# Seven half-size products instead of eight for gate and up in a float32 decoder trunk on TensorE

## The chip, the cores and the metric

The kernel runs on one core of a Trainium2 chip. TensorE multiplies a stationary operand of 128 x 128 with a moving operand of up to 512 columns and adds into PSUM. VectorE, ScalarE and GpSimd work beside it, each with a queue of its own, and the queue of SyncE issues most transfers. The metric is the device time of one execution in microseconds, as the median of several runs.

## The reference

The input x has 512 positions and 1024 features. There are two layers. Each adds a half SwiGLU stage, a mixer (retention and dilated attention in layer 0, gated linear attention in layer 1), and a second half SwiGLU stage; a last norm follows. All is float32. The change touches the four SwiGLU stages:

```python
def _swiglu(h, wg, wu, wd):
    return (jax.nn.silu(h @ wg) * (h @ wu)) @ wd
...
    for l in range(DEPTH):
        h = _rmsnorm(x, ffn_pre_norm[l])
        x = x + 0.5 * _swiglu(h, ffn_pre_w_gate[l], ffn_pre_w_up[l], ffn_pre_w_down[l])
...
```

wg and wu are 1024 x 2816, wd is 2816 x 1024.

## The kernel before

Activations lie transposed: x is eight tiles of 128 features x 512 positions that stay in SBUF. The hidden width of 2816 is 22 tiles of 128, or 11 pairs of tiles. To keep float32 accuracy each operand is cut into a high half (a float32r copy, made on ScalarE) and a low half (the difference, made on VectorE), and each 128 x 128 by 128 x 512 product is three matmuls into the same PSUM tile: high by high, high by low, low by high. `mm3` (L121) issues the three; they are L124, L125 and L126 in the profile.

Weights come through one ordered plan (`run`, L756). `weights` (L77) takes the next tile and keeps LOOK = 3 more ahead: `load_w` (L83) transfers 512 KB on SyncE's queue, casts the high half `whi` on ScalarE (L89) and subtracts for the low half `wlo` on VectorE (L90). `whi` and `wlo` have four buffers each.

A SwiGLU stage (`ffn`, L292) works in two phases. For each of 22 tiles `proj_t` (L242) makes the gate tile and then the up tile, each 8 x 3 = 24 matmuls of 512 columns on x scaled by the norm's gain only (`xgh`, `xgl`, made by `scaled`, L165). `glu` multiplies both by `rrow`, the row of reciprocal norms per position, takes Silu, multiplies, and cuts the result into `act` halves. The row is not needed before `glu`, so the first projections run while it is made: `squares` (L182) sums x squared on GpSimd while the stage before ends, `stats_cols` (L220) and `stats_rows` (L224) are hooked in after the first two projections (third and fourth in the first stage). `rows` (L205) spreads it with two small `diag` matmuls. Then come the eight down tiles: `down` (L331) adds 22 products x 3 matmuls in one PSUM tile, `x` is updated (L326), and the next stage's scaled copy is made at once. The last output tile of the program runs in two halves of 256 columns (`last_half`, L339), so that the first half's final norm and stores run beside the second half.

Who comes first on an engine is set by the layer that records the program: it lists the instructions engine by engine, in an order of its own that keeps to what depends on what. Every engine then works through its list in that order.

## Time and profile before

| | |
|---|---|
| median of 3 runs | 1969.83 us (1969.54 to 1972.41) |
| the profiled execution | 1968.25 us |
| its span in the profile | 1966.3 us |
| TensorE busy, matmuls | 1949.1 us (99%), 8822 records |
| VectorE / ScalarE / GpSimd busy | 898.9 / 611.6 / 97.4 us |
| granted TensorE clock | 0.998 of full speed |
| HBM read | 179.89 MB, 93 GB/s over the span |

Matmuls are pipelined: a record's duration reaches into the next ones, so the time of a matmul is read from the distance between two starts. A few per cent of matmul records can be missing. Idle time of an engine that is off the path costs nothing.

### The profile page before, as it was taken

What the parts mean: (1) busy time and instruction counts of PE and PEld (TensorE: products, weight loads), DVE (VectorE), ACT (ScalarE), POOL (GpSimd) and SP (SyncE); (2) the same over time, 40 slices, a digit from 0 to 9 for tenths busy, and PEclk for the clock granted to TensorE, in tenths of its full rate; (3) what the DMA queues carried; (4) which work ended last, traced back from release to release, by engine and by line L of the source; (5) the groups of instructions that cost most, each with busy time, mean ns of one, the idle gap of its engine ahead of it and who ended that gap; (6) DMA issues with size and microseconds to landing.
All of it is one profiled execution on the core that took longest, in us unless ns stands there. A gap on an engine that the chain in (4) does not pass through costs nothing.

```text
span 1966.3 us, 21475 instructions
## 1 busy us (share of the span) xinstructions
PE 1949.1 (99%) x8822; PEld 1595.4 (81%) x8822; DVE 898.9 (46%) x1238; ACT 611.6 (31%) x813; POOL 97.4 (5%) x69
## 2 busy tenths in 40 slices
PE   8999999999999999999999999999999999999998
PEld 7888888877777888888888888888788888888887
DVE  6444433544565544443334444333456564444323
ACT  5333322233332332322233323222424243333221
POOL 1000001100001200000110000011000020000010
PEclk9999999999999999999999999999999999999999
DMA  5232233421121323222332332233222133223222
GB/s 173 97 97 97 94 98 92 140 81 57 54 70 49 118 96 97 97 94 96 95 102 97 97 97 96 89 99 104 91 84 67 55 117 97 97 97 95 92 95 73
DMA packets 54548, 183.38 MB, mean 93 GB/s; under 512 B 6177, under 2 KB 8481, under 8 KB 54450
## 3 DMA queue, kind: packets, MB, share of 16 engines
q1 hardware_dynamic: 51408, 177.76, 28.0%
q10 hardware_dynamic: 3042, 4.26, 0.7%
q8 instruction: 69, 1.13, 0.2%
q14 instruction: 29, 0.24, 0.0%
HBM read 179.89 MB, written 2.10 MB: 93 GB/s over the span
## 4 chain that ended last, share of the span: by engine, by line
PE 98%; issue 0%; DVE 0%; DMA 0%; POOL 0%; ACT 0%; POOLq 0%; DVEq 0%; SPq 0%
PE pj L124 31%; PE pj L126 30%; PE pj L125 30%; PE sc L520 1%; PE o L548 1%; PE sc L199 1%; PE sc L595 0%; PE tp L536 0%; PE sc L217 0%; PE o L752 0%; PE o L745 0%; PE sc L734 0%; DMA wraw<-in_w_gu 0%; PE tp L604 0%; PE o L124 0%
## 5 line engine op out<-in xcount | busy, mean ns | idle before, releaser
L89 ACT CAST whi<-wraw 128x1024 fp32r<-128x1024 f32 (+1 forms) x341 | 352.1, 1033 | 1112.1 <-PE pj L125 670.2
L124 PE MATMUL pj<-xgh,whi 128*128 128x512 f32 x1704 | 677.4, 398 | 6.9 <-ACT whi L89 6.9
L126 PE MATMUL pj<-xgh,wlo 128*128 128x512 f32 x1704 | 664.8, 390 | 0.0
L125 PE MATMUL pj<-xgl,whi 128*128 128x512 f32 x1704 | 664.6, 390 | 0.0
L90 DVE TENSOR_TENSOR wlo<-wraw,whi 128x1024 fp32r<-128x1024 f32 (+1 forms) x341 | 412.6, 1211 | 297.2 <-ACT whi L89 296.2
L124 PEld LDWEIGHTS pj<-xgh,whi 128*128 128x128 f32 x1704 | 320.6, 188 | 83.2 <-issue 12.1
L126 PEld LDWEIGHTS pj<-xgh,wlo 128*128 128x128 f32 x1704 | 320.2, 188 | 67.7 <-DVE wlo L90 0.8
L125 PEld LDWEIGHTS pj<-xgl,whi 128*128 128x128 f32 x1704 | 320.7, 188 | 64.3 <-issue 1.0
L124 PE MATMUL pj<-acth,whi 128*128 128x512 f32 (+1 forms) x726 | 277.8, 383 | 0.0
L125 PE MATMUL pj<-actl,whi 128*128 128x512 f32 (+1 forms) x726 | 277.7, 383 | 0.0
L126 PE MATMUL pj<-acth,wlo 128*128 128x512 f32 (+1 forms) x726 | 277.7, 383 | 0.0
L303 DVE TENSOR_TENSOR us<-pj,rrow 128x512 f32<-128x512 f32 x88 | 60.8, 691 | 272.4 <-PE pj L126 272.4
L124 PEld LDWEIGHTS pj<-acth,whi 128*128 128x128 f32 x726 | 136.4, 188 | 26.8
L126 PEld LDWEIGHTS pj<-acth,wlo 128*128 128x128 f32 x726 | 136.4, 188 | 26.5
L125 PEld LDWEIGHTS pj<-actl,whi 128*128 128x128 f32 x726 | 136.4, 188 | 26.5
L189 POOL TENSOR_TENSOR sqa<-sqa,sq 128x512 f32<-128x512 f32 x41 | 71.3, 1738 | 1412.4 <-issue 795.4
L301 DVE TENSOR_TENSOR gs<-pj,rrow 128x512 f32<-128x512 f32 x88 | 60.8, 691 | 173.7 <-PE pj L126 173.7
L117 ACT CAST acth<-us 128x512 fp32r<-128x512 f32 x88 | 54.9, 624 | 61.0 <-DVE us L304 61.0
L304 DVE TENSOR_TENSOR us<-us,gs 128x512 f32<-128x512 f32 x88 | 60.9, 692 | 9.4 <-ACT gs L302 0.8
L118 DVE TENSOR_TENSOR actl<-us,acth 128x512 fp32r<-128x512 f32 x88 | 60.3, 685 | 4.9 <-ACT acth L117 4.8
L326 DVE SCALAR_TENSOR_TENSOR x<-pj,x 128x512 f32<-128x512 f32 x31 | 21.4, 692 | 88.3 <-PE pj L126 88.3
L302 ACT ACTIVATE gs<-gs 128x512 f32<-128x512 f32 x88 | 55.2, 628 | 4.2 <-DVE gs L301 4.2
(164 smaller groups left out, 1170.1 us busy)
## 6 DMA issues: line engine op xcount, KB each, us to landing
wraw<-in_w_gu SPq DMA_DIRECT2D x176, 512.0 KB, 3.4
wraw<-in_w_down SPq DMA_DIRECT2D x64, 448.0 KB, 3.2
wraw<-in_w_down SPq DMA_DIRECT2D x32, 512.0 KB, 3.4
wraw<-in_w_dqk SPq DMA_DIRECT2D x8, 512.0 KB, 3.4
wraw<-in_w_rqk SPq DMA_DIRECT2D x8, 512.0 KB, 3.4
wraw<-in_w_eo SPq DMA_DIRECT2D x8, 512.0 KB, 3.6
wraw<-in_w_gr SPq DMA_DIRECT2D x8, 512.0 KB, 3.4
wraw<-in_w_gv SPq DMA_DIRECT2D x8, 512.0 KB, 3.5
```

The costliest lines, as they stand in the source:

```text
L89: self.halved = nc.scalar.copy(out=hi[:, :cols], in_=raw[:, :cols]).ins
L90: nc.vector.tensor_tensor(out=lo[:, :cols], in0=raw[:, :cols], in1=hi[:, :cols].bitcast(F32), op=ALU.subtract)
L117: nc.scalar.copy(out=hi, in_=src)
L118: nc.vector.tensor_tensor(out=lo, in0=src, in1=hi.bitcast(F32), op=ALU.subtract)
L124: mm(out, lhsT=w[0], rhs=x[0], start=first, stop=False)
L125: mm(out, lhsT=w[0], rhs=x[1], start=False, stop=False)
L126: self.last = mm(out, lhsT=w[1], rhs=x[0], start=False, stop=last).ins
L189: nc.gpsimd.tensor_tensor(out=self.sqacc, in0=self.sqacc, in1=sq, op=ALU.add)
L301: nc.vector.tensor_tensor(out=gs, in0=g, in1=self.rrow, op=ALU.mult)
L302: nc.scalar.activation(out=gs, in_=gs, func=AF.Silu)
L303: nc.vector.tensor_tensor(out=us, in0=u, in1=self.rrow, op=ALU.mult)
L304: nc.vector.tensor_tensor(out=us, in0=us, in1=gs, op=ALU.mult)
```

## The change

Gate and up of the tile pairs 2 to 10 are now made as 2 x 2 blocks: the weight is four quarters of 512 x 128 (two halves of the 1024 inputs by the two tiles of the pair), the activations are four quarters of 512 inputs x 256 positions. By Winograd's form of Strassen's method a block takes seven products of quarter sums instead of eight products of quarters. `product` issues 4 x 3 = 12 matmuls of 256 columns for each. `block` adds them up: four go one after another into `a`, which is copied out to `part` on ScalarE after each of the first three; the other three go into the two halves of `b`; VectorE adds the copies to `b`. The sums of weight quarters are made on VectorE for each block (`block_plan`: two quarters are cut as they are, then four sums and one more quarter), from one transfer of 1 MB. The sums of activation quarters are made once for each stage (`moving`), from x times gain times `rrow`, so that Silu needs no further scaling; seven pieces x four row pairs, high and low. `ahead` and `room` prepare the six weight operands of a block up to one block ahead, beside the plain tiles.

Pairs 0 and 1 (HEAD = 2) run as before, while the row of norms and then `moving` are made. Activations of a group of pairs are kept in nine `xgh`/`xgl` buffers that `scaled` shares, and the down sum is added to x in six groups of pairs, five of them as tiles between the products of the next pairs (`fill`, `down_tile`), the last one at the end (`last_group`). `rrow` and `diag` have one buffer instead of two, and the scratch for DMA descriptors is set to 1024.

```diff
+AHEAD, SUMS = 4, 6
 HELD = 4
 PASS3 = 0.65
-DOWN_SPLIT = ((0, 8), (8, 15), (15, 22))
+H = T // 2
+HEAD = 2
+GROUPS = ((0, 1), (2, 3), (4, 5), (6, 7), (8,), (9, 10))
+BLOCKS = ((2, 3), (4, 5), (6, 7), (8, 9), (10,))
+XGB = 9
...
@@ weights
...
+        while self.plan and self.room(self.plan[0][0]):
+            self.ahead()
+        return self.ready.pop(0)[1]
+    def ahead(self):
+        kind, step = self.plan.pop(0)
+        self.ready.append((kind, step()))
+    def room(self, kind):
+        n = sum(k == kind for k, _ in self.ready)
+        return n <= LOOK if kind == "w" else n < AHEAD and len(self.ready) < AHEAD + 2
...
@@ block_plan
...
+        def high(key, x):
+            if not self.spaced:
+                self.spaced = True
+                self.t2k(self.fpool, "space", bufs=1, shape=[P, 16])
+            hi = self.t2k(self.fpool, "shi", F32R, SUMS, shape=[P, T])
+            nc.scalar.copy(out=hi, in_=x)
+            st[key] = (hi, x)
+        def low(key):
+            hi, x = st[key]
+            lo = self.t2k(self.fpool, "slo", F32R, SUMS, shape=[P, T])
+            nc.vector.tensor_tensor(out=lo, in0=x, in1=hi.bitcast(F32), op=ALU.subtract)
+            return hi, lo
+        def add(out, a, b):
+            nc.vector.tensor_tensor(out=out, in0=a, in1=b, op=ALU.add)
+        def c0():
+            raw = st["raw"] = self.t2k(self.fpool, "raw", shape=[P, 4 * T], bufs=2)
+            nc.sync.dma_start(out=raw, in_=src)
+            hi = self.t2k(self.wpool, "whi", F32R, shape=[P, WC])
+            lo = self.t2k(self.wpool, "wlo", F32R, shape=[P, WC])
+            nc.scalar.copy(out=hi, in_=raw[:, :WC])
+            st["s3"] = self.t2k(self.fpool, "s3", bufs=1)
+            add(st["s3"], raw[:, q[0]], raw[:, q[2]])
+            add(raw[:, q[2]], raw[:, q[2]], raw[:, q[3]])
+            high("s1", raw[:, q[2]])
+            nc.vector.tensor_tensor(out=lo, in0=raw[:, :WC], in1=hi.bitcast(F32), op=ALU.subtract)
+            add(raw[:, q[0]], raw[:, q[0]], raw[:, q[2]])
+            return hi, lo
+        def s1():
+            high("s2", st["raw"][:, q[0]])
+            return low("s1")
+        def s2():
+            raw = st["raw"]
+            high("s3", st["s3"])
+            add(raw[:, q[1]], raw[:, q[1]], raw[:, q[0]])
+            return low("s2")
+        def s3():
+            high("a22", st["raw"][:, q[3]])
+            return low("s3")
+        def a22():
+            high("s4", st["raw"][:, q[1]])
+            return low("a22")
+        def s4():
+            return low("s4")
+        return [("w", c0), ("s", s1), ("s", s2), ("s", s3), ("s", a22), ("s", s4)]
...
@@ moving, product, block
...
+    def moving(self, g):
+        nc = self.nc
+        for k in range(KD // 2):
+            b = self.t2k(self.fpool, "sg", bufs=2, shape=[P, 2 * T]).rearrange("p (s t) -> p s t", t=H)
+            d = self.t2k(self.fpool, "sg", bufs=2, shape=[P, 2 * T]).rearrange("p (s t) -> p s t", t=H)
+            two = lambda x: x.rearrange("p (s t) -> p s t", t=H)
+            for kk, out in ((k, b[:, 0::3, :]), (k + KD // 2, b[:, 1:3, :])):
+                gain = self.gain[:, g * KD + kk: g * KD + kk + 1]
+                nc.vector.scalar_tensor_tensor(out=out, in0=two(self.x[kk]), scalar=gain, in1=two(self.rrow), op0=ALU.mult, op1=ALU.mult)
+            hi = self.t2k(self.fpool, "hh", F32R, KD // 2, shape=[P, 7 * H])
+            lo = self.t2k(self.fpool, "hl", F32R, KD // 2, shape=[P, 7 * H])
+            h3, l3 = two(hi), two(lo)
+            nc.scalar.copy(out=h3[:, :3, :], in_=b[:, :3, :])
+            nc.vector.tensor_tensor(out=d[:, 0:2, :], in0=b[:, 0::2, :][:, :2, :], in1=b[:, 3:4, :].broadcast_to([P, 2, H]), op=ALU.subtract)
+            sub = dict(scalar=-1.0, op0=ALU.mult, op1=ALU.subtract)
+            nc.vector.scalar_tensor_tensor(out=d[:, 2, :], in0=d[:, 1, :], in1=b[:, 0, :], **sub)
+            nc.vector.scalar_tensor_tensor(out=d[:, 3, :], in0=d[:, 2, :], in1=b[:, 1, :], **sub)
+            nc.scalar.copy(out=h3[:, 3:, :], in_=d)
+            nc.vector.tensor_tensor(out=l3[:, :3, :], in0=b[:, :3, :], in1=h3[:, :3, :].bitcast(F32), op=ALU.subtract)
+            nc.vector.tensor_tensor(out=l3[:, 3:, :], in0=d, in1=h3[:, 3:, :].bitcast(F32), op=ALU.subtract)
+            self.hs.append((hi, lo))
+            yield
+    def product(self, out, w, at, slot, first):
+        ts = slice(slot * H, (slot + 1) * H)
+        mm = self.nc.tensor.matmul
+        for k in range(KD // 2):
+            s = slice(at + k * P, at + (k + 1) * P)
+            hi, lo = (x[:, ts] for x in self.hs[k])
+            mm(out, lhsT=w[0][:, s], rhs=hi, start=first and k == 0, stop=False, skip_group_check=True)
+            mm(out, lhsT=w[0][:, s], rhs=lo, start=False, stop=False, skip_group_check=True)
+            self.last = mm(out, lhsT=w[1][:, s], rhs=hi, start=False, stop=k == KD // 2 - 1, skip_group_check=True).ins
+    def block(self, fill):
+        nc = self.nc
+        a, b = self.psum("pj"), self.psum("pj")
+        part = self.t2k(self.fpool, "part", bufs=2, shape=[P, 3 * H])
+        save = lambda i: nc.scalar.copy(out=part[:, i * H:(i + 1) * H], in_=a[:, :H])
+        c0 = self.weights()
+        self.product(a[:, :H], c0, 0, 0, True)
+        save(0)
+        self.product(b[:, H:], self.weights(), 0, 3, True)
+        self.product(a[:, :H], self.weights(), 0, 5, False)
+        save(1)
+        self.product(b[:, :H], c0, T, 1, False)
+        self.product(a[:, :H], self.weights(), 0, 4, False)
+        save(2)
+        nc.vector.tensor_tensor(out=part[:, 2 * H:], in0=b[:, H:], in1=part[:, 2 * H:], op=ALU.add)
+        fill()
+        self.product(a[:, :H], self.weights(), 0, 6, False)
+        self.product(b[:, H:], self.weights(), 0, 2, False)
+        nc.vector.tensor_tensor(out=part[:, :T], in0=b, in1=part[:, :T], op=ALU.add)
+        fill()
+        return a, part
...
@@ ffn
...
+            for n in range(2 * HEAD):
+                held.append((n, self.proj_t(), self.proj_t()))
+                if n > 0:
+                    head()
+                    next(build, None)
+                    next(build, None)
+            head()
+            for sg in heads:
+                self.keep_act(sg)
...
+            for before, group in zip(GROUPS, BLOCKS):
+                calls = 4 * len(group)
+                order = [KD * (i + 1) // calls - KD * i // calls for i in range(calls)]
+                tiles = iter(range(KD))
+                share = iter(order)
+
+                def fill():
+                    for _ in range(next(share)):
+                        self.down_tile(next(tiles), before, False, nxt)
+
+                for p in group:
+                    sg = new_sg()
+                    a, c = self.block(fill)
+                    nc.scalar.activation(out=sg[:, :T], in_=c[:, :T], func=AF.Silu)
+                    nc.scalar.activation(out=sg[:, T:T + H], in_=a[:, :H], func=AF.Silu, scale=-1.0)
+                    nc.scalar.activation(out=sg[:, T + H:], in_=c[:, T:], func=AF.Silu, scale=-1.0)
+                    a, c = self.block(fill)
+                    neg = dict(scalar=-1.0, op0=ALU.mult, op1=ALU.mult)
+                    nc.vector.tensor_tensor(out=sg[:, :T], in0=c[:, :T], in1=sg[:, :T], op=ALU.mult)
+                    nc.vector.scalar_tensor_tensor(out=sg[:, T:T + H], in0=a[:, :H], in1=sg[:, T:T + H], **neg)
+                    nc.vector.scalar_tensor_tensor(out=sg[:, T + H:], in0=c[:, T:], in1=sg[:, T + H:], **neg)
+                    self.keep_act(sg)
+            self.last_group(GROUPS[-1], nxt)
...
+    def down_tile(self, d, group, final, nxt):
+        nc = self.nc
+        w, at = self.chunk(d, group)
+        ps = self.psum("pj")
+        acts = self.act[2 * group[0]:2 * group[-1] + 2]
+        self.down_mm(ps, w, at, acts, slice(0, T), True, True)
+        nc.vector.scalar_tensor_tensor(out=self.x[d], in0=ps, scalar=0.5, in1=self.x[d], op0=ALU.mult, op1=ALU.add)
...
@@ last_group
+                if nxt is not None and e < XGB - n:
+                    self.scaled(e, nxt)
+                self.squares(e)
+            first = []
+        if nxt is not None:
+            for e in range(XGB - n, KD):
+                self.scaled(e, nxt)
...
@@ rows
-            diag = self.t2k(self.misc, "diag", F32R, bufs=2)
+            diag = self.t2k(self.misc, "diag", F32R, bufs=1)
```

Three places show how the lists of the engines change.

TensorE, in a stage's gate and up work. Before: one projection, five of its 24 rows, `pj` the PSUM tile and `wlo`/`whi` the weight's halves.

```order
L126 MATMUL pj_5573<-xgh_4385,wlo_5457 128x512
L124 MATMUL pj_5573<-xgh_4395,whi_5456 128x512
L125 MATMUL pj_5573<-xgl_4396,whi_5456 128x512
L126 MATMUL pj_5573<-xgh_4395,wlo_5457 128x512
L124 MATMUL pj_5573<-xgh_4406,whi_5456 128x512
```

Now: the end of a block's fifth product, the third into `a` (here `pj_6293`), then a down tile `pj_6387`. `hh`/`hl` are the halves of `moving`'s pieces, `shi`/`slo` those of a weight sum.

```order
L405 MATMUL pj_6293<-hl_6024,shi_6222 128x256
L406 MATMUL pj_6293<-hh_6023,slo_6255 128x256
L404 MATMUL pj_6293<-hh_6036,shi_6222 128x256
L405 MATMUL pj_6293<-hl_6037,shi_6222 128x256
L406 MATMUL pj_6293<-hh_6036,slo_6255 128x256
L205 MATMUL pj_6387<-xgh_6116,whi_6259 128x512
L206 MATMUL pj_6387<-xgl_6117,whi_6259 128x512
L207 MATMUL pj_6387<-xgh_6116,wlo_6260 128x512
L205 MATMUL pj_6387<-xgh_6120,whi_6259 128x512
```

Narrow matmuls have taken the place of wide ones, and down tiles stand between products, so the width changes within a block.

ScalarE, in the same work. Before: a weight cast for each projection, with a Silu or a cast of `act` between two of them.

```order
L89 CAST whi_5240<-wraw_5238 128x1024
L117 CAST acth_5347<-us_5342 128x512
L89 CAST whi_5281<-wraw_5279 128x1024
L302 ACTIVATE gs_5413<-gs_5413 128x512
L89 CAST whi_5312<-wraw_5310 128x1024
L117 CAST acth_5419<-us_5414 128x512
L89 CAST whi_5353<-wraw_5351 128x1024
```

Now: one block. The three COPY rows move `a` (`pj_6293`) to `part`; the casts of `shi` and `whi` are for the block after it, those of `xgh` are its own activations.

```order
L414 COPY part_6295<-pj_6293 128x256
L125 CAST shi_6364<-raw_6327 128x512
L125 CAST shi_6382<-s_1176_6332 128x512
L414 COPY part_6295<-pj_6293 128x256
L142 CAST whi_6498<-raw_6496 128x1024
L125 CAST shi_6413<-raw_6327 128x512
L414 COPY part_6295<-pj_6293 128x256
L125 CAST shi_6465<-raw_6327 128x512
L125 CAST shi_6504<-raw_6496 128x512
L438 CAST xgh_6453<-sg_6132 128x512
L438 CAST xgh_6457<-sg_6132 128x512
L106 CAST whi_6588<-wraw_6586 128x1024
```

Between the copies, on each of which a product waits, stand casts for later work.

VectorE, at the start of a stage, once `rrow` is there. Before: `glu` for one tile and the low halves of weights (L90) between its steps.

```order
L301 TENSOR_TENSOR gs_4837<-pj_4678,rrow_4670 128x512
L90 TENSOR_TENSOR wlo_4706<-wraw_4703,whi_4705 128x1024
L303 TENSOR_TENSOR us_4838<-pj_4709,rrow_4670 128x512
L304 TENSOR_TENSOR us_4838<-us_4838,gs_4837 128x512
L90 TENSOR_TENSOR wlo_4737<-wraw_4734,whi_4736 128x1024
L118 TENSOR_TENSOR actl_4844<-us_4838,acth_4843 128x512
L301 TENSOR_TENSOR gs_4909<-pj_4740,rrow_4670 128x512
```

Now, at the start of the second stage: `glu` (L451 to L454), and between its steps the pieces of `moving` (L383 to L394), of which four such sets are made.

```order
L451 TENSOR_TENSOR head_5904<-pj_5765,rrow_5840 128x512
L453 TENSOR_TENSOR part_5905<-pj_5805,rrow_5840 128x512
L383 SCALAR_TENSOR_TENSOR sg_5910<-x_82,gain,rrow_5840 128x2x256
L454 TENSOR_TENSOR head_5904<-part_5905,head_5904 128x512
L383 SCALAR_TENSOR_TENSOR sg_5910<-x_86,gain,rrow_5840 128x512
L439 TENSOR_TENSOR xgl_6117<-head_5904,xgh_6116 128x512
L388 TENSOR_TENSOR sg_5911<-sg_5910 128x512
L393 TENSOR_TENSOR hl_5915<-sg_5910,hh_5914 128x768
L107 TENSOR_TENSOR wlo_5876<-wraw_5873,whi_5875 128x1024
L390 SCALAR_TENSOR_TENSOR sg_5911<-sg_5911,sg_5910 128x256
L451 TENSOR_TENSOR head_5904<-pj_5848,rrow_5840 128x512
L391 SCALAR_TENSOR_TENSOR sg_5911<-sg_5911,sg_5910 128x256
```

The work on the activations' quarters stands in one list with the low halves of the weights that TensorE reads next.

## Rows read from the trace of the kernel before

**Rows 1.** the page, parts 1 and 4: engines' busy time; chain that ended last
```profile
PE 1949.1 (99%) x8822; PEld 1595.4 (81%) x8822; DVE 898.9 (46%) x1238; ACT 611.6 (31%) x813; POOL 97.4 (5%) x69
...
PE 98%; issue 0%; DVE 0%; DMA 0%; POOL 0%; ACT 0%; POOLq 0%; DVEq 0%; SPq 0%
```

**Rows 2.** groups by shape, TensorE: xcount, busy us, mean ns, idle before
```profile
L124 PE MATMUL pj<-xgh,whi 128*128 128x512 f32 x1704 | 677.4, 398 | 6.9 <-ACT whi L89 6.9
...
L124 PE MATMUL pj<-acth,whi 128*128 128x256 f32 x44 | 12.5, 285 | 0.0
...
L126 PEld LDWEIGHTS pj<-xgh,wlo 128*128 128x128 f32 x1704 | 320.2, 188 | 67.7 <-DVE wlo L90 0.8
```

**Rows 3.** timeline of TensorE, last down tiles: start us, duration us, what
```profile
1936.04 0.39 PE L124 MATMUL pj<-acth,whi 128*128 128x512 f32 x1
...
1938.76 0.28 PE L124 MATMUL pj<-acth,whi 128*128 128x256 f32 x1
...
1939.11 0.28 PE L124 MATMUL pj<-acth,whi 128*128 128x256 f32 x1
...
1945.11 0.28 PE L126 MATMUL pj<-acth,wlo 128*128 128x256 f32 x1
```

**Rows 4.** timeline of TensorE, after a row of norms, and the mixer's end
```profile
375.99 0.48 PE L124 MATMUL pj<-xgh,whi 128*128 128x512 f32 x1
...
376.31 0.39 PE L125 MATMUL pj<-xgl,whi 128*128 128x512 f32 x1
...
640.01 0.40 PE L124 MATMUL pj<-cath,whi 128*128 128x512 f32 x1
...
652.61 0.40 PE L124 MATMUL pj<-cath,whi 128*128 128x512 f32 x1
```

**Rows 5.** groups by shape, VectorE and ScalarE
```profile
L90 DVE TENSOR_TENSOR wlo<-wraw,whi 128x1024 fp32r<-128x1024 f32 x277 | 342.7, 1238 | 95.0 <-ACT whi L89 94.8
...
L172 DVE SCALAR_TENSOR_TENSOR xgl<-x,gain,xgh 128x512 fp32r<-128x512 f32 x48 | 39.7, 841 | 4.2 <-ACT xgh L171 4.2
...
L346 DVE SCALAR_TENSOR_TENSOR x<-pj,x 128x256 f32<-128x256 f32 x2 | 0.8, 425 | 7.2 <-PE pj L126 7.2
...
L117 ACT CAST acth<-us 128x512 fp32r<-128x512 f32 x88 | 54.9, 624 | 61.0 <-DVE us L304 61.0
...
L302 ACT ACT_TABLE_LOAD x1 | 1.3, 1283 | 1.5 <-DVE gs L301 1.5
...
L538 ACT COPY pt<-tp 128x256 f32<-128x256 f32 x8 | 2.9, 364 | 8.1 <-PE tp L536 8.0
```

**Rows 6.** timeline of VectorE in a feed-forward stage
```profile
206.73 0.69 DVE L303 TENSOR_TENSOR us<-pj,rrow 128x512 f32<-128x512 f32 x1 [3.31 <-PE pj L126]
207.53 0.69 DVE L304 TENSOR_TENSOR us<-us,gs 128x512 f32<-128x512 f32 x1
208.14 1.22 DVE L90 TENSOR_TENSOR wlo<-wraw,whi 128x1024 fp32r<-128x1024 f32 x1
```

**Rows 7.** chain of waits in order of time: start us, us, what
```profile
5.77 1.05 ACT whi L89
...
6.87 0.80 PE pj L124
...
32.14 0.47 PE sc L217 x2
```

**Rows 8.** timeline of ScalarE: rows of norms of the first two feed-forward stages
```profile
33.93 0.58 ACT L227 COPY rrow<-sc 128x512 f32<-128x512 f32 x1
...
666.13 0.58 ACT L227 COPY rrow<-sc 128x512 f32<-128x512 f32 x1
```

**Rows 9.** timeline: TensorE's first matmul of the second stage; VectorE, last update
```profile
653.31 0.40 PE L124 MATMUL pj<-xgh,whi 128*128 128x512 f32 x1
...
1955.90 0.42 DVE L346 SCALAR_TENSOR_TENSOR x<-pj,x 128x256 f32<-128x256 f32 x1
```

**Rows 10.** DMA issues: count, KB each, median us to landing
```profile
wraw<-in_w_gu SPq DMA_DIRECT2D x176, 512.0 KB, 3.4
```

More of the change, by code (lines that the diff above doesn't have):

```diff
@@ L147, in setup @@
             if k == 0:
-                self.ready.append(self.load_w(*self.plan.pop(0)))
+                self.ahead()
         for _ in range(2):
-            self.ready.append(self.load_w(*self.plan.pop(0)))
+            self.ahead()
         with self.tc.tile_pool(name="start", bufs=1, reuse_waits="tile") as pool:
@@ new lines, in keep_act, with ffn, glu, head @@
+    def keep_act(self, sg):
+        for i in range(2):
+            hi = self.t2k(self.xg, "xgh", F32R)
+            lo = self.t2k(self.xg, "xgl", F32R)
+            x = sg[:, i * T:(i + 1) * T]
+            nc = self.nc
+            nc.scalar.copy(out=hi, in_=x)
+            nc.vector.tensor_tensor(out=lo, in0=x, in1=hi.bitcast(F32), op=ALU.subtract)
+            self.act.append((hi, lo))
+    def ffn(self, f, nxt):
+        nc, tc = self.nc, self.tc
+        gi = (0, 2, 3, 5)[f]
+        with tc.tile_pool(name=self.uid("ffn"), bufs=1, reuse_waits="tile") as self.fpool, self.banks(pj=7, sc=1):
+            self.act, self.hs, self.spaced = [], [], False
+            new_sg = lambda: self.t2k(self.fpool, "sg", bufs=2, shape=[P, 2 * T])
+            def glu(g, u, out):
+                us = self.t2k(self.fpool, "part", bufs=2, shape=[P, 3 * H])[:, :T]
+                nc.vector.tensor_tensor(out=out, in0=g, in1=self.rrow, op=ALU.mult)
+                nc.scalar.activation(out=out, in_=out, func=AF.Silu)
+                nc.vector.tensor_tensor(out=us, in0=u, in1=self.rrow, op=ALU.mult)
+                nc.vector.tensor_tensor(out=out, in0=us, in1=out, op=ALU.mult)
+            held, heads = [], []
+            build = self.moving(gi)
+            def head():
+                n, g, u = held.pop(0)
+                if n % 2 == 0:
+                    heads.append(self.t2k(self.fpool, "head", shape=[P, 2 * T], bufs=1) if n == 0 else new_sg())
+                glu(g, u, heads[-1][:, n % 2 * T:(n % 2 + 1) * T])
+            for n in range(2 * HEAD):
[28 more added lines that the diff above has]
+            self.last_group(GROUPS[-1], nxt)
@@ new lines, in down_mm, with chunk @@
+    def down_mm(self, ps, w, at, acts, ts, first, last):
+        for i, (hi, lo) in enumerate(acts):
+            s = slice(at + i * P, at + (i + 1) * P)
+            self.mm3(ps, (w[0][:, s], w[1][:, s]), (hi[:, ts], lo[:, ts]), first and i == 0, last and i == len(acts) - 1)
+    def chunk(self, d, group):
+        n = 2 * len(group) * P
+        per = WC // n
+        if d % per == 0:
+            self.dw = self.weights()
+        return self.dw, d % per * n
+    def down_tile(self, d, group, final, nxt):
+        nc = self.nc
+        w, at = self.chunk(d, group)
[3 more added lines that the diff above has]
+        nc.vector.scalar_tensor_tensor(out=self.x[d], in0=ps, scalar=0.5, in1=self.x[d], op0=ALU.mult, op1=ALU.add)
@@ new lines, in last_group @@
+    def last_group(self, group, nxt):
+        nc = self.nc
+        acts = self.act[2 * group[0]:2 * group[-1] + 2]
+        n, m = len(acts), len(acts) - 2
+        first = []
+        for d in range(KD):
+            w, at = self.chunk(d, group)
+            if nxt is None and d == KD - 1:
+                self.pending = []
+                for half in range(2):
+                    self.last_half(d, w, at, acts, slice(half * T // 2, (half + 1) * T // 2))
+                while self.pending:
+                    self.hook()
+                break
+            ps = self.psum("pj")
+            first.append((d, w, at, ps))
+            if d < 3:
+                self.down_mm(ps, w, at, acts[:m], slice(0, T), True, False)
+            if d < 2:
+                continue
+            for e, w, at, ps in first:
+                if e < 3:
+                    self.down_mm(ps, w, at + m * P, acts[m:], slice(0, T), False, True)
+                else:
+                    self.down_mm(ps, w, at, acts, slice(0, T), True, True)
+                nc.vector.scalar_tensor_tensor(out=self.x[e], in0=ps, scalar=0.5, in1=self.x[e], op0=ALU.mult, op1=ALU.add)
+                if nxt is not None and e < XGB - n:
+                    self.scaled(e, nxt)
+                self.squares(e)
+            first = []
+        if nxt is not None:
+            for e in range(XGB - n, KD):
+                self.scaled(e, nxt)
@@ L770, in run @@
         for h in range(RET_HEADS):
[L771 removed]
+            self.plan += [one(a["w_rg"][h], WC)] + (qk("w_rqk", h + 2, 4) if h < 2 else [])
         self.plan += tiles(a["w_eo"])
```

111 lines of the change are left out of this document (46 added, 65 removed).

## The prediction

> **What bounds the kernel now.** I read the page's first part and its chain of waits first. TensorE is busy in 99% of the span and 98% of the chain that ended last is its own matmuls [rows 1]; no other engine is above 46%. So the time is the number of matmuls times their spacing, and another engine counts only where it makes TensorE wait. Next I read the groups by shape: gate and up projections are wide matmuls (512 columns), and 256-column ones stand only in the last output tile [rows 2]. Each has its own weight load of 188 ns [rows 2]. The durations (398 ns, 285 ns) overlap, so the price is the distance from start to start, read from the timeline of the last 30 us. From 1936.04 to 1938.76 stand 12 wide matmuls: 2.72/12 = 0.2267 us. From 1939.11 to 1945.11 stand 50 narrow ones: 6.00/50 = 0.1200 us [rows 3]. Half the columns cost 53%, not 50%: 512 columns more or less are 0.2133 us, and 13.3 ns per matmul stay whatever the width.
>
> **The matmuls.** A pair of tiles of gate (or of up) took 2 x 8 x 3 = 48 wide matmuls. It now takes seven products of 4 x 3 = 12 narrow ones, 84. There are 9 pairs x 2 x 4 feed-forward stages = 72 such blocks. Removed: 3456 x 0.2267 = 783.4 us. Added: 6048 x 0.1200 = 725.8 us. Difference -57.6 us. One eighth of the columns would be 97.9 us at the old price per column; 40 us of that goes to the fixed part of more, shorter matmuls. The first two pairs and the down sum keep their matmuls. Of the last output tile, which ran in halves as 132 narrow matmuls, only 24 remain narrow and 54 become wide: 15.84 us to 15.12 us, -0.7.
> The nearest row for another price of a narrow matmul is that same run; for a worse one I use the wide matmuls at the end of the even mixer, where 54 gaps from 640.01 to 652.61 are 0.2333 us each, 6.7 ns above the others, with no wait [rows 4]. I take 0.1200 and keep 0.1267 for the range; a gain below 0.1200 I bound at 1 ns, the reading error of 50 rows, or 6 us.
> The Trainium skill speaks against this change: "TensorE: Matmul & The Clock Gate", Part 3, says that a weight load runs beside a matmul in flight only where the row groups differ, and here every load takes all rows. By that rule a matmul would cost its load and its columns one after the other, 0.188 + 0.227 before and 0.188 + 0.120 after, and the change would add 6048 x 0.308 - 3456 x 0.415 = 429 us. The spacing of 0.2267 and 0.1200 us with loads of 188 ns in between [rows 2, 3] denies it, and the sum goes by the spacing.
>
> **Changing width.** Each block goes from narrow to wide and back twice (two down tiles within it). After short matmuls the trace shows a first wide gap of 0.32 us instead of 0.23 (375.99 to 376.31) [rows 4]; from wide to narrow (1938.76) it shows none. 144 changes x 0.09 = 13 us, and 1728 wide matmuls at the slower step 12 us, bound it above; nothing below. Those short ones had one column, these have 256, so I stay nearer the lower end: +5.
>
> **Start of a stage.** The blocks multiply normed activations, so the row of norms must be there and `moving` must build seven half-size pieces, in high and low halves, of four row pairs on VectorE. In the first stage the row ends at 34.5 [rows 8]. TensorE is past the fourth projection at 32.14 + 0.47 [rows 7] and has four more at 24 x 0.2267 = 5.44 us: it wants the first block at 54.4. The order lists 44 VectorE instructions between the row and the last low half that the first two products read. By the mean durations (1.24 us for 1024 elements, 0.69 for 512, 0.84 with a gain, about 0.43 for 256 [rows 5, 6]) that is 34 us; by start-to-start distances (independent 0.61, dependent 0.80 [rows 6]) about 30. One activation table load of 1.3 us [rows 5] is also waited for. The last half is ready at about 66.6, and TensorE has some 5 us of other work to put ahead of it (two products and pieces of a down tile): a stall of about 8, bounds 5 to 11. In the other three stages the row comes 13.4 us after the stage's first matmul (653.31 to 666.71 [rows 8, 9]) and the blocks are wanted at 44.8 (eight projections, 1.3 for the norms). Here 46 instructions stand ahead, 32.3 to 36.7 us: ready at 46 to 51, wanted at 47.3 after two and three quarter products. 0 to 5 each, taken 1.7. Together +13, bounds 5 to 26.
>
> **The blocks.** One pair costs TensorE 2 x (84 x 0.12) + 48 x 0.2267 = 31.0 us. VectorE: per block four sums of weight blocks, five low halves, two wide low halves, two sums out of PSUM and two x updates, 11.2 us, and 3.0 more in the up block: 25.4 us per pair, 82%. ScalarE: 15.3, 49% (1.05 per wide cast [rows 7], 0.62 per half cast, 0.36 for a copy of 256 columns [rows 5]). Neither is the bound by its sum. What counts is the loop TensorE, ScalarE, TensorE: `a` is copied out three times before the next product is added to it. A copy may start 0.16 (duration less spacing [rows 3]) plus about 0.05 after the product's last matmul, and TensorE may go on 0.05 after its end (6.82 to 6.87 [rows 7]). The first copy has one product of 1.44 us as cover; the third has a down tile of 2.72. The second is tight: the order puts two casts between the first copy and it, and the second of them reuses a buffer that the same product has just read. So ScalarE has 0.2 + 0.62 + 0.36 + 0.05 = 1.23 us to go against 1.44: 0.2 us to spare. Weights are prepared one block ahead, and the 1 MB transfer (512 KB landed in 3.4 us [rows 10], so at most 6.8) has 8.5 us from the freeing of its buffer to its first reader: hidden. I take +0.1 us per block for lateness that I cannot see, +7; bounds 0 and 0.4 (29).
>
> **Ends of stages.** The tail: half 1's update starts at 1955.90 and the span ends 10.4 us later [rows 9]. Half 0's chain of norms, rows and stores ran beside 66 matmuls (7.9 us); it now has 12 (1.44 us), and VectorE does both halves' 3.2 us of stores one after the other: +3, bounds 0 to 6. The scaled copies of the last three x tiles now wait for the activations' buffers. They come 3 to 5 us after the last down matmul and are wanted at 3.4, 4.1 and 4.8: 0.5 us per stage. `diag` with one buffer makes the second half of a row of norms wait for the first matmul, some 0.1 us in each of 16 calls. Together +3, bounds 0 to 6. The freed DMA scratch moves nothing in this program's order.
>
> **Sum.** -57.6 - 0.7 + 5 + 13 + 7 + 3 + 3 = -27.3 on the profiled execution's 1968.25 (span 1966.3 and 1.95 around it) = 1941. The median of the runs lies 1.6 above that execution, so I forecast 1943 us.
>
> **Rivals.**
> 1. The copies hold TensorE. ScalarE works in order; if one wide cast (1.05 us) stands ahead of the second copy when its product ends, the 0.2 us are gone and TensorE stands 0.85 us in each of 72 blocks: 61 us instead of 7, 1943 + 54 = 1997. For it: that queue waits for VectorE and for TensorE itself, and one late sum of weights delays everything behind it. Against: ScalarE has half its time free. It decides from 0.48 us per block on, (7.2 + 27.3)/72. 7%.
> 2. Mixed widths run at the slower step seen after the mixer: 6.7 ns x (6048 + 1728) = 52 us and 13 for the changes, less the 5 in the sum: 1943 + 60 = 2003. For it: the step lasted 12 us there without any wait, after a stage of mixed shapes [rows 4]. Against: in the last tile, wide and narrow follow each other at the better step [rows 3]. It decides from 4 ns per matmul. 6%.
> 3. Start stalls at their upper bound and half of 1 or 2: the gain is spent, 1965 to 1975. 6%.
> 4. The serial rule: weight loads do not hide and the time is about 2400. By the rule of "TensorE: Matmul & The Clock Gate" quoted above; the trace has it otherwise at both widths, 1%.
>
> **Chances and range.** The forecast, 80%; its own range is 1918 to 1962: 25 us less of the 31 that the last five terms add (the start's lower bound stays) to 19 more. The upper part of the 8 in 10 must reach into 1 and 3: 1918 to 1980. A measurement of this kernel tells 0.2% (4 us) from no change. Faster by more than that: 0.81 (the forecast and a little of 3). Within it: 0.04 (from 3). Slower: 0.15 (1, 2, 4, the rest of 3).
>
> **What would show it.** In the changed kernel's profile: narrow matmuls at 0.120 us within a product, and about 725 us for all; TensorE's idle time by releaser below 35 us, most of it for `hh` and `hl` in the first block of each stage, about 8 us in the first and under 5 in the others; nearly none for `part` copies; VectorE near 80% within the blocks. I am wrong in the first step if the narrow spacing is 0.125 or more, in the third if the starts cost over 26 us, in the fourth if the second copy's wait is a steady row of the waits.

## The result: 1921.94 us, a gain almost twice the forecast

The changed kernel takes 1921.94 us (median of 4 runs, 1918.82 to 1923.64); the kernel before, on the same chip, 1971.09. The ratio is 0.9749, 95% interval 0.9732 to 0.9766. The forecast was 1943 in a range of 1918 to 1980. The profiled execution took 1920.47 us with a span of 1918.7: 47.6 less than the span of before, where the forecast's sum had 27.3.

### The profile page after: what moved, and what is told of

It is laid out like the page before. It is cut to its first block, busy times and chain, and to the rows that moved or that the text cites. A ratio compares the mean times of both kernels' runs of the same rounds, so it can differ in the third digit from the quotient of the medians.

```text
span 1918.7 us, 28135 instructions
## 1 busy us (share of the span) xinstructions
PE 1889.4 (98%) x11360; PEld 1660.4 (87%) x11360; DVE 1383.0 (72%) x2114; ACT 850.2 (44%) x1377; POOL 90.1 (5%) x69
## 4 chain that ended last, share of the span: by engine, by line
PE 95%; DVE 3%; issue 1%; ACT 0%; POOL 0%; DMA 0%; POOLq 0%; DVEq 0%; SPq 0%; ACTq 0%
PE pj L205 17%; PE pj L206 17%; PE pj L207 17%; PE pj L404 12%; PE pj L406 12%; PE pj L405 12%; PE sc L740 1%; PE o L768 1%; PE sc L280 1%; PE sc L298 0%; PE sc L815 0%; PE tp L756 0%; DVE xgl L253 0%; DVE wlo L107 0%; PE o L972 0%
## 5 line engine op out<-in xcount | busy, mean ns | idle before, releaser
L405 PE MATMUL pj<-hl,shi 128*128 128x256 f32 x1440 | 404.9, 281 | 1.5 <-DVE hl L394 1.5
L404 PE MATMUL pj<-hh,shi 128*128 128x256 f32 x1440 | 405.0, 281 | 0.8 <-ACT hh L392 0.8
L406 PE MATMUL pj<-hh,slo 128*128 128x256 f32 x1440 | 404.7, 281 | 0.0
L106 ACT CAST whi<-wraw 128x1024 fp32r<-128x1024 f32 x189 | 197.8, 1047 | 254.2 <-PE pj L206 164.1
L125 ACT CAST shi<-raw 128x512 fp32r<-128x512 f32 x288 | 178.5, 620 | 288.1 <-PE pj L405 232.6
L107 DVE TENSOR_TENSOR wlo<-wraw,whi 128x1024 fp32r<-128x1024 f32 x189 | 236.1, 1250 | 65.5 <-ACT whi L106 64.9
L406 PEld LDWEIGHTS pj<-hh,slo 128*128 128x128 f32 x1440 | 276.6, 192 | 0.1
L405 PEld LDWEIGHTS pj<-hl,shi 128*128 128x128 f32 x1440 | 270.5, 188 | 4.6 <-DVE hl L394 1.7
L404 PEld LDWEIGHTS pj<-hh,shi 128*128 128x128 f32 x1440 | 270.5, 188 | 4.0 <-ACT hh L392 1.1
L131 DVE TENSOR_TENSOR slo<-raw,shi 128x512 fp32r<-128x512 f32 x288 | 197.1, 687 | 83.4 <-ACT shi L125 83.3
```

The source lines that it names most:

```text
L106: self.halved = nc.scalar.copy(out=hi[:, :cols], in_=raw[:, :cols]).ins
L107: nc.vector.tensor_tensor(out=lo[:, :cols], in0=raw[:, :cols], in1=hi[:, :cols].bitcast(F32), op=ALU.subtract)
L125: nc.scalar.copy(out=hi, in_=x)
L131: nc.vector.tensor_tensor(out=lo, in0=x, in1=hi.bitcast(F32), op=ALU.subtract)
L404: mm(out, lhsT=w[0][:, s], rhs=hi, start=first and k == 0, stop=False, skip_group_check=True)
L405: mm(out, lhsT=w[0][:, s], rhs=lo, start=False, stop=False, skip_group_check=True)
```

## The profile after

Three lines of the page: part 1, part 4, and from part 5 the first group of narrow matmuls (count, busy us, mean ns, idle time before):

```profile
PE 1889.4 (98%) x11360; PEld 1660.4 (87%) x11360; DVE 1383.0 (72%) x2114; ACT 850.2 (44%) x1377; POOL 90.1 (5%) x69
...
PE 95%; DVE 3%; issue 1%; ACT 0%; POOL 0%; DMA 0%; POOLq 0%; DVEq 0%; SPq 0%; ACTq 0%
...
L404 PE MATMUL pj<-hh,shi 128*128 128x256 f32 x1440 | 405.0, 281 | 0.8 <-ACT hh L392 0.8
```

Against [rows 1], TensorE is still the bound (95% of the chain); VectorE rose from 46% to 72%. TensorE's seven longest waits by releaser (total in us, times, longest):

```profile
PE pj L205 <- ACT whi L106: 7.1, 1, 7.1
PE sc L298 <- DVE diag L296: 5.5, 6, 1.8
PE sc L280 <- DVE x L578: 3.4, 1, 3.4
PE pj L405 <- DVE hl L394: 1.5, 1, 1.5
PE pj L205 <- ACT cath L198: 1.5, 1, 1.5
PE pj L206 <- DVE xgl L253: 1.0, 1, 1.0
PE sc L280 <- POOL sqa L270: 0.8, 1, 0.8
```

The first is the program's start, as in [rows 7]. No row names a `part` copy: the blocks wait for nothing. The price of a narrow matmul, which [rows 3] gave as 0.1200, is read from the blocks' segment of the second stage, its first and last narrow matmul:

```profile
690.53 0.28 PE L404 MATMUL pj<-hh,whi 128*128 128x256 f32 x1
...
963.69 0.28 PE L406 MATMUL pj<-hh,slo 128*128 128x256 f32 x1
```

273.16 us, in which stand 420 wide matmuls (95.2 us at 0.2267) and 1511 steps of narrow ones: 177.96/1511 = 0.1178 us each, changes of width included. The segments of the third and fourth stage are 273.16 too. The first runs from 55.28 to 336.38, 281.10 us. In it TensorE waits for the moving pieces that VectorE builds, and from 61.05 on its matmuls take longer (narrow ones, 0.28 elsewhere, up to 0.58):

```profile
58.21 0.39 PE L404 MATMUL pj<-hh,shi 128*128 128x256 f32 x1 [0.77 <-ACT hh L392]
60.07 0.38 PE L405 MATMUL pj<-hl,shi 128*128 128x256 f32 x1 [1.47 <-DVE hl L394]
61.33 0.80 PE L205 MATMUL pj<-xgh,whi 128*128 128x512 f32 x1 [0.77 <-DVE part L453]
62.80 0.58 PE L405 MATMUL pj<-hl,whi 128*128 128x256 f32 x1 [0.46 <-DVE hl L393]
```

At the end, the first half's eight stores on VectorE, and TensorE's norms of the second half behind them:

```profile
1895.55 0.28 PE L205 MATMUL pj<-xgh,whi 128*128 128x256 f32 x1
...
1903.17 0.58 PE L298 MATMUL sc<-diag,ones_r 128*128 128x256 f32 x1 [0.52 <-DVE diag L296]
...
1903.88 3.22 DVE L578 SCALAR_TENSOR_TENSOR x<-x,gain,sc 128x256 f32<-128x256 f32 x8 [0.76 <-PE sc L298]
...
1907.15 0.58 PE L280 MATMUL sc<-ones,sqa 128*128 128x1 f32 x2 [3.39 <-DVE x L578]
```

From the last tile's first narrow matmul to the span's end, less its narrow matmuls at 0.12, were 1966.3 - 1938.76 - 132 x 0.12 = 11.7 us [rows 3]; now 1918.7 - 1895.55 - 24 x 0.12 = 20.3. And where the second stage passes into the third:

```profile
992.80 1.39 POOL L270 TENSOR_TENSOR sqa<-sqa,sq 128x512 f32<-128x512 f32 x1 [2.02 <-ACT sq L266]
993.31 1.44 DVE L253 SCALAR_TENSOR_TENSOR xgl<-x,gain,xgh 128x512 fp32r<-128x512 f32 x1 [0.24 <-ACT xgh L252]
994.80 0.50 PE L206 MATMUL pj<-xgl,whi 128*128 128x512 f32 x1 [0.98 <-DVE xgl L253]
```

`xgl` takes 1.44 us beside GpSimd's addition; its median is 0.75. Six stretches: these waits of the first stage, the slower part of them, nearly the whole of that stage's segment, ahead of and behind the late `xgl`, and the second stage's blocks (us; busy and count of PE, PEld, DVE, ACT, POOL; granted clock; DMA share; GB/s):

```profile
58.20:65.00 6.80, 3.82 (x10) 2.38 (x11) 6.80 (x12) 1.79 (x2) 0.00 (x0) 0.71 0.24 77
61.05:67.88 6.83, 5.81 (x15) 4.19 (x16) 6.83 (x12) 3.06 (x6) 0.00 (x0) 0.50 0.00 0
56.00:336.00 280.00, 276.26 (x1924) 257.84 (x1923) 220.20 (x329) 131.03 (x225) 0.00 (x0) 0.99 0.28 100
...
993.80:996.20 2.40, 1.42 (x12) 1.31 (x11) 0.95 (x1) 0.86 (x1) 0.40 (x1) 1.00 0.66 222
996.20:999.60 3.40, 3.40 (x10) 2.67 (x10) 2.08 (x5) 0.19 (x1) 1.02 (x1) 0.52 0.00 0
...
690.50:963.70 273.20, 273.20 (x1933) 256.80 (x1932) 211.41 (x314) 128.84 (x222) 0.00 (x0) 1.00 0.30 104
```

In the first two VectorE is busy throughout, and TensorE's granted clock is 0.71 and 0.50 (the lower level, 1.2 GHz). In the second, 15 matmuls keep TensorE busy for 5.81 us; 7 wide and 8 narrow ones at their usual steps are 2.5. So of the 7.9 us by which the first stage's segment is longer, 3.3 went to matmuls at the lower clock, and most of the rest is TensorE's idle time, 280.00 - 276.26 = 3.7 us in the third stretch. After the 2.4 us of the fourth stretch, with TensorE 1.4 us busy, the granted clock was 0.52 again: eight wide matmuls 0.43 apart, 1.65 us lost. In the blocks VectorE is busy 211.4/273.2 = 77%.

## The experiments

Theory going in: TensorE alone bounds the blocks; the narrow matmul is cheaper than I priced it, for a reason to be found. Rivals: the copies of `a` or VectorE hold part of the gain back; 0.1178 is a property of the seven products.

**Narrow matmuls without the seven products.** In the kernel before, gate and up of 9 pairs run over 256 columns at a time (`cols` holds the two halves; the rest of the calls is left out here):

```
+        for ts in self.cols:
             for k in range(KD):
-                self.mm3(ps, ..., self.h[k], ...)
+                self.mm3(ps[:, ts], ..., [x[:, ts] for x in self.h[k]], ...)
```

> The kernel before, with one edit: gate and up of 9 of 11 pairs run their eight row tiles first over the left 256 columns, then over the right 256. So 3456 wide matmuls become 6912 narrow ones, nothing else changes, and no product is saved. Theory A (narrow matmuls cost 0.1178 us wherever they stand in long runs, as in the blocks of the changed kernel): 6912 x 0.1178 - 783.4 = +31 us, 2002. Theory B (the price of my prediction, 0.1200, holds for halves of a 512-column tile, and 0.1178 is particular to the seven products' operands): +46 us, 2017. In both the idle time of TensorE stays as before, and the difference to the changed kernel's time is what the seventh-eighths saving itself brings.

Measured 2016.03 us, ratio 1.0238 [1.0222, 1.0253]: theory B. First and last narrow matmul of a stage, and ahead of them a run of wide ones:

```profile
676.92 0.39 PE L127 MATMUL pj<-xgh,whi 128*128 128x512 f32 x1
...
709.56 0.28 PE L127 MATMUL pj<-xgh,whi 128*128 128x256 f32 x1
...
916.79 0.28 PE L129 MATMUL pj<-xgh,wlo 128*128 128x256 f32 x1
```

207.23/1727 = 0.1200 us for narrow, 32.64/144 = 0.2267 for wide. Narrowness alone costs 47 us; something made the products' matmuls cheaper.

**An eighth product.** `self.product(b[:, H:], w7, 0, 2, False)` stands twice.

> The changed kernel, with the seventh product of each block run twice (12 narrow matmuls more in each of 72 blocks, the output differs by that). If TensorE alone bounds the blocks and a narrow matmul costs 0.1178 us: 864 x 0.1178 = +101.8 us, 2024. If another engine or the weights' loop were the bound in the blocks, part of it would vanish in its shadow: clearly under +100. Against the kernel before with halves only (eight eighths by the old route) it should stand higher by what starts, ends and tail of the new route cost, some 20 us.

Measured 2021.84 us, ratio 1.0268 [1.0250, 1.0285]; spans 2020.2 against 1918.7, +101.5. The blocks' segments of stages 2 to 4 grew by 25.44 us, 25.44/216 = 0.1178. TensorE is the bound with nothing in its shadow. The expectation's last sentence did not hold: over the halves it stands 6 us higher, not 20, as the old route's 6912 narrow matmuls cost 2.2 ns more each, 15 us.

**Casts ahead of the second copy.** Two copies from the block's `whi` stand ahead of `save(1)` in the code.

> The changed kernel, with two idle half-width ScalarE copies (0.62 us each, 0.53 from start to start) put ahead of the second copy of `a` in each of 72 blocks, about 1.1 us. By my prediction's reckoning (0.2 us to spare) TensorE would stand some 0.9 us per block: +65 us, 1987. By the trace of the changed kernel, where the second copy ends 0.79 us ahead of the matmul that needs it: 1.1 - 0.75 = 0.35 us per block, +25 us, 1947. If the copies were hidden by something else altogether: 1922. The wait then shows on the first matmul of the product on slot 4, on the part copy.

Measured 1919.57 us, ratio 0.9748 [0.9733, 0.9762], nothing lost. It was no test: the casts depend only on weights that are there early, and the program's scheduling put them where ScalarE was idle, as between a wide cast and the third copy:

```profile
803.63 1.05 ACT L142 CAST whi<-raw 128x1024 fp32r<-128x1024 f32 x1 [0.52 <-PE pj L405]
804.72 0.62 ACT L421 COPY sq<-whi 128x512 f32<-128x512 f32 x1
805.25 0.37 ACT L414 COPY part<-pj 128x256 f32<-128x256 f32 x1
```

**Copies that cannot go early.**

```
+        for _ in range(3):
+            nc.scalar.copy(out=..."sq"...[:, :H], in_=a[:, :H])
         save(1)
```

> The changed kernel with three more copies of the same 256 columns of `a` (to a scratch buffer, 0.37 us each) directly ahead of the second copy in each of 72 blocks; they need the product that the second copy needs, so no idle time of ScalarE can take them earlier. The trace of the changed kernel has the second copy end 0.4 us ahead of its reader in one block looked at; three more take 0.85 to 1.1. Theory of my prediction (the loop TensorE, ScalarE, TensorE is what counts, 0.2 us to spare): 0.65 to 0.9 us in each block, +47 to +65. With 0.4 us to spare: 0.45 to 0.7, +32 to +50, about 1963, and the wait on the part copies as a row of TensorE's waits. If nothing waits for these copies: 1922.

Measured 1929.85 us, ratio 0.9787 [0.9770, 0.9803]: +8, 0.11 us per block (7.9/72): less than a loop with 0.2 or 0.4 us to spare would lose, and more than nothing. The wait is there, small:

```profile
805.69 0.40 ACT L414 COPY part<-pj 128x256 f32<-128x256 f32 x1
805.71 0.39 PE L205 MATMUL pj<-xgh,whi 128*128 128x512 f32 x1
805.93 0.39 PE L206 MATMUL pj<-xgl,whi 128*128 128x512 f32 x1
...
806.14 0.19 PEld L404 LDWEIGHTS pj<-hh,shi 128*128 128x128 f32 x1 [0.24 <-ACT part L414]
```

Two wide matmuls of a down tile now stand ahead of the waiting product: the order on TensorE is planned too, and gave the late copy cover. So the copies are a real link in a loop, with more room than I read from the order of one kernel.

**The tile `space`.** The diff holds a tile of 64 bytes that nothing reads, ahead of `shi` and `slo`. By the addresses in the built programs, weight and moving buffers of [rows 3] and of the halves lie 0 apart (mod 128 bytes). Those of the products lie 64 apart: on `shi` and `slo` (five products of seven) through this tile, on `whi` and `wlo` also without it.

```
-    self.t2k(self.fpool, "space", bufs=1, shape=[P, 16])
```

> The changed kernel without the unused 64-byte tile `space` that its block plan puts ahead of the buffers shi and slo. It only moves those twelve buffers down by 64 bytes: with it the address of a weight (mod 128) lies 64 from that of the moving piece it meets, without it 0; the two products per block that read whi and wlo keep their 64. Theory A (the price of a narrow matmul hangs on this address relation: the halves of the first experiment and the last tile, all at 0, ran at 0.1200, the blocks at 64 ran at 0.1178): five of seven products go to 0.1200, 4320 x 0.0022 = +9.6 us, 1931. Theory B (it is something else in the products): 0.1178 stays and the time too, 1922.

Measured 1935.82 us, ratio 0.9817 [0.9802, 0.9832]: +13.9. The second stage's segment:

```profile
693.67 0.28 PE L404 MATMUL pj<-hh,whi 128*128 128x256 f32 x1
...
970.51 0.28 PE L406 MATMUL pj<-hh,slo 128*128 128x256 f32 x1
```

276.84 us in place of 273.16. Within products that read `shi` the step went from 0.1177 to 0.1198 (990 steps, 2.06 us), and within those on `whi` it stayed (0.1177 and 0.1178). That is theory A: 8.2 us in four stages, of 9.6 expected. But 1.56 of the 3.68 us are in the 420 wide matmuls of the down tiles, which went from 0.2267 to 0.2304 although their own buffers did not move, some 6 us in four stages. A down tile of 12, from its first matmul to the next narrow one, takes 2.77 us in place of 2.72:

```profile
700.81 0.39 PE L205 MATMUL pj<-xgh,whi 128*128 128x512 f32 x1
...
703.58 0.28 PE L404 MATMUL pj<-hh,shi 128*128 128x256 f32 x1
```

Theory A did not foresee this part, and no run explains it.

The next two runs have a tile of 128 bytes (`shape=[P, 32]`) and of 192 (`[P, 48]`):

> The changed kernel with `space` of 128 bytes in place of 64: the weights of shi and slo lie 0 (mod 128) and 128 (mod 256) from the moving pieces. Theory A with a period of 128 bytes: as without the space, five of seven products at 0.1200, 1931. With a longer period another price shows in those products, above or below 0.1178. Theory B: no change, 1922.

> The changed kernel with `space` of 192 bytes: shi and slo 192 bytes (64 mod 128) from the moving pieces; whi and wlo keep 64. With a period of 128 bytes the blocks' segments of stages 2 to 4 stay at 273.16 us, 1922. If 64 bytes is a value of its own and 192 like 128 (273.96 each), 1 to 3 us more; if the price repeats otherwise, up to the 276.84 of the kernel without the space, 1936.

Measured 1925.47 us (0.9763 [0.9748, 0.9777]) and 1917.69 (0.9737 [0.9720, 0.9755]); segments 273.96 and 272.17. The second stage's segment and its mean steps (us):

| bytes of `space` | segment | within products on `shi` | on `whi` | wide |
|---|---|---|---|---|
| 0 | 276.84 | 0.1198 | 0.1178 | 0.2304 |
| 64 | 273.16 | 0.1177 | 0.1177 | 0.2267 |
| 128 | 273.96 | 0.1184 | 0.1157 | 0.2289 |
| 192 | 272.17 | 0.1169 | 0.1156 | 0.2288 |

A period of 128 does not hold. Products on `whi` and wide matmuls changed too, though their own addresses did not move, so the relation of one weight to its moving piece is not the whole rule. What the rule is stays open.

**The halves, 64 bytes apart.** An unused 64-byte tile between `xg` and `wpool`, in the first experiment's kernel.

> The first experiment's kernel (the kernel before with gate and up of 9 pairs in halves of 256 columns), with an unused tile of 64 bytes between the activations' buffers and the weights', so that their addresses lie 64 (mod 128) apart instead of 0. Theory A (the address relation sets the price of a narrow matmul whatever route it comes from): 6912 narrow ones go from 0.1200 to 0.1178, -15 us. The wide projections from the same buffers (768 in the stages, some 700 in the mixers) get the relation too; the mixers' output matmuls, wide ones at 64, ran at 0.2333 against 0.2267, so up to +10 there: 2001 to 2011. Theory B (0.1178 belongs to the products, and the 64 bytes acted there through something else): 2016 or above.

Measured 2009.38 us (2016.03 without), ratio 1.0183 [1.0157, 1.0210]:

```profile
676.75 0.39 PE L128 MATMUL pj<-xgh,whi 128*128 128x512 f32 x1
...
710.34 0.28 PE L128 MATMUL pj<-xgh,whi 128*128 128x256 f32 x1
...
913.74 0.28 PE L130 MATMUL pj<-xgh,wlo 128*128 128x256 f32 x1
```

Narrow: 203.40/1727 = 0.1178, from 0.1200. Wide: 33.59/144 = 0.2333, from 0.2267. The same 64 bytes make one cheaper by 2.2 ns and the other dearer by 6.6. The relation acts at both widths and without any product: theory A. In the built programs weight and moving buffers lie at 0 and 0 (mod 128) in the halves (0.1200), at 64 and 0 in the halves with the pad (0.1178), at 0 and 64 in the products (0.1177), and at 64 and 64 in those on `shi` without `space` (0.1198). So in these four cases neither address alone made the difference; their distance did. One thing stays open: the four runs took 2009.70, 2000.93, 2009.18 and 2009.58 us at the same granted clock of 0.998. Only the first of them has a trace, so why one was 8 us shorter isn't known.

**Down tiles ahead of the first block.** First stage only: its eight first down tiles run between the last projection and the first block, with two steps of `moving` (`build`) among them.

```
+            if f == 0:
+                self.early(GROUPS[0], build)
```

> The changed kernel, with the down tiles of the first group of the first stage (21.8 us of TensorE) put between the last projection and the first block; the moving pieces are built one row pair per projected pair and the rest beside those tiles. Theory: the 7.9 us that the first stage's block segment is longer than the others' is waiting for the moving halves, so it goes: 1914. Rival: the activations of the first two pairs come late as well (the same row of norms, and two row pairs of pieces ahead of them on VectorE), and 3 to 8 us of it stay as a wait for xgl ahead of the down tiles: 1917 to 1922.

Measured 1913.17 us, ratio 0.9718 [0.9703, 0.9732]; the span fell by 7.8, and the rows of `hh` and `hl` left TensorE's waits, as the theory had it. The lower clock in this stage (61.05 to 67.88 before) went with them. What came in their place, 0.5 us in blocks without a down tile to cover the copy:

```profile
PE pj L404 <- ACT part L414: 0.5, 2, 0.3
```

**The tail.** Rows of norms in banks of the seven; the second half's chain among the first half's stores.

```
-            row.append(self.rows(col, "sc", n // P))
+        rows = lambda: row.append(self.rows(col, "pj", n // P))
...
+            self.pending = [cols, early0, rows, late0, early, late]
```

> The changed kernel with another order in the last output tile: each half's row of norms has a bank of the seven, not the single `sc` bank, and the second half's norms and row stand among the first half's stores on VectorE, not behind all eight. In the changed kernel TensorE waits 3.4 us there for a store of the first half. Theory: the wait goes and the second half's stores start 3 to 4 us sooner, 1918. Rival: the stores themselves and the last transfers set the end (VectorE's sixteen stores, 6.4 us, in a row behind the first row), then at most 2 us: 1920 to 1922.

Measured 1917.19 us, ratio 0.9725 [0.9710, 0.9739]. The span shows only 1.0 less, as the second mixer, ahead of the fourth stage, took 3.2 us more: the granted clock fell to 0.50 in it. From the blocks' last matmul to the end it is 1917.7 - 1876.78 = 40.9 us against 1918.7 - 1873.68 = 45.0. The norms no longer wait for a store (first the stretch at the lower clock, then the tail):

```profile
1354.81:1361.64 6.83, 6.83 (x14) 3.92 (x13) 0.00 (x0) 5.06 (x6) 0.00 (x0) 0.50 0.25 79
...
1905.51 0.42 PE L280 MATMUL sc<-ones,sq 128*128 128x1 f32 x2
...
1907.32 1.66 DVE L578 SCALAR_TENSOR_TENSOR x<-x,gain,pj 128x256 f32<-128x256 f32 x4 [0.34 <-PE pj L298]
```

**Together**, with two buffers of `diag`; and then with `cath` and `catl` moved to 0 (mod 512) from the weights.

> The changed kernel with both edits that paid (the first stage's first down tiles ahead of its first block, the last tile's norms in banks of their own and among the stores) and two buffers of `diag` in place of one. If the gains add: -7.9, -4.1, and 1 to 2 for `diag` (TensorE waits 5.5 us for it in all, in six places, of which the tail holds a part): about 1909. If the second and third are the same wait: 1911.

> The kernel of the run before it, with unused tiles of 64 and 384 bytes ahead of the mixers' buffers `cath` and `catl`, so that they lie 0 (mod 512) from the weights they meet, as the activations of the stages do. If the address relation sets the price of a wide matmul too, the 384 wide matmuls of the two output stages go from 0.2333 to 0.2267: -2.6 us, about 1906 against 1909. If the slower step belongs to something else in the mixers: no change.

Measured 1904.41 us (0.9670 [0.9654, 0.9686]) and 1903.92 (0.9666 [0.9649, 0.9682]). The first beats both kernels: 65 us below before, 17.5 below the changed one, some 4 more than the 13 to 14 expected. The profiled executions differ by 15.5: 7.7 in the first stage, 5.0 in the tail and 2.3 in the two mixers. The second can't be told from the first by time; its output matmuls went from 0.2331 (355 steps) to 0.2275 (354), which over 384 of them is 2.2 us, as expected in kind. By the built programs these buffers had lain 64 bytes apart in the first mixer and 384 (mod 512) in the second, and both had the dearer step (0.2332 and 0.2329), so 64 is not the only distance that has it.

## Why the prediction was right in kind and short in size

The working held: TensorE bounds the blocks, and seven narrow products for eight wide ones set the sign. By term, forecast and measured (us):

| term | forecast | measured |
|---|---|---|
| 6048 narrow for 3456 wide | -57.6 | -70.9 (6048 x 0.1178 - 783.4) |
| last tile's matmuls | -0.7 | -0.7 |
| changing width | +5 | 0 (inside the 273.16) |
| starts of stages | +13 | +7.9 (281.10 - 273.16) in the first; 0 in the others' blocks |
| blocks | +7 | 0 |
| tail | +3 | +8.6 (20.3 - 11.7) |
| ends of stages, mixers, rest | +3 | +7.5 (what is left) |
| sum | -27.3 | -47.6 |

- **The matmuls' price is the step that failed.** I took 0.1200 from the last tile and allowed 1 ns below it; it was 2.2 ns below. The row was right for its place: the halves ran at 0.1200 in 6912 matmuls. But the change also moved buffers, by a tile in the diff that I passed over. That tile is worth 13.9 us: 8.2 in the narrow matmuls of five products, the other part mainly in wide matmuls that would else be slower. The two products on `whi` lie 64 apart without it too.
- **Rival 2 misread its row.** The 0.2333 of the mixer's end [rows 4] is no after-effect of mixed shapes: moving a buffer by 64 bytes made the same step in plain projections, and moving `cath` took most of it away (0.2275).
- **Changing width and blocks were caution.** Both had 0 as a bound. For the blocks I took one kernel's order on ScalarE as fixed; the order on all engines is planned around a delay, as the three copies showed.
- **The first stage's 8 us were right** in size, and the last low half that the first two products read was ready at 66.36 us, where I had 66.6. But I took the whole of it for idle time. TensorE stood for 3.7 us, and 3.3 went to matmuls at the lower clock, for which the sum has no term; how much the clock cost by itself no run separates, as the early down tiles removed both. The other stages had their pieces in time. My 47.3 for them is 44.8 and one and three quarter products, not two and three quarters; nothing hangs on it.
- **The tail was outside its bounds** (0 to 6). I counted VectorE's stores and the lost cover, but not that the diff leaves one `sc` bank where there were two: the second half's norms wait for the bank that the first half's stores read. With a bank of the seven and another order, 4.1 us come back; which of the two edits gave them no run separates.
- **Ends of stages** were outside their bounds too (0 to 6). 3.4 of the 7.5 are the third stage's start (a slow `xgl`, then the lower clock) and 2.8 the two mixers: 284.4 and 221.0 us, where they had been 283.6 and 219.0. With two buffers of `diag` they are 283.8 and 219.3, and without that edit the early down tiles leave them at 284.4 and 221.1, so the single `diag` buffer, which I priced at 0.1 us a call, cost 2.3 there.
- **The total is partly luck.** 1921.94 lies in the range, but the price came out 13.3 us better than forecast, where I allowed 6, and tail and ends of stages 10.1 worse together. Of the 25 us that I had set aside for width, starts and blocks, 17.1 were not needed. These together make the 20.3 us between forecast and measurement.
- The serial weight load (rival 4) stayed away: at 0.1178 us per matmul the loads of 188 ns still lie beside other matmuls. The rule of different row groups that I quoted from Part 3 of "TensorE: Matmul & The Clock Gate" in the Trainium skill would have it otherwise; by that rule the time would be about 2400, and the runs decide against it here. The same part of the Trainium skill also lets a load go ahead of matmuls where it targets the background weight buffer. The overlap seen here agrees with that, but whether these loads do so no run shows.

## What to carry to other kernels

Price a matmul at the addresses that it will have: read the step from a long run in the same buffers, and ask of every unused tile in a diff whom it moves. Where a program's order is planned, a cost put in by hand may be hidden again, so make it depend on what the suspected instruction depends on. When a loop loses its cover, count the banks as well as the engines.

## What the runs showed of the hardware

- In the halves, 64 bytes between weight and moving buffers change TensorE's step in opposite directions by width: 256 columns 0.1200 to 0.1178 us, 512 columns 0.2267 to 0.2333, with no wait and the granted clock at 1.00. In the changed kernel, steps also changed of matmuls whose own buffers stayed where they were (wide ones 0.2267 to 0.2304), so the rule is not known.
- VectorE's `xgl` took 1.44 us beside a GpSimd addition on SBUF, 0.75 in the median. Of its 48 rows in the changed kernel, the 18 that started while such an addition ran ended some 0.55 us after its end, and the other 30 took 0.74 to 0.75. "Trainium Architecture — The Big Picture" in the Trainium skill (What this means for kernel authors) says that on the engines' side of SBUF only VectorE and GpSimd contend, for a port pair that one of them holds at a time; these rows agree.
- One short lull of TensorE (1.4 us busy in 2.4) was followed by 3.4 us at a granted clock of 0.52. Such a stretch came at the third stage's start (near 997) or in the second mixer (near 1358) in some runs and not in others: at both in the tail's kernel, at neither in that of the casts. It cost 1.6 us at the stage's start (48.35 us up to its first block, against 46.71 without it) and 3.2 in the mixer (224.2 against 221.0).
